# Two-head score pairs in two row halves, and decay rows read back from DRAM, in a two-layer hybrid backbone

## The chip, the cores and the metric

The kernel runs on one core of a Trainium2 chip. The metric is the device time of one execution in microseconds (us). The engines are TensorE (PE, with its weight loads PEld), VectorE (DVE), ScalarE (ACT), GpSimd (POOL) and SyncE (SP), which here issues the DMAs. Each works through its own queue in order.

## The reference, cut to what matters

Two layers over 256 latent and 256 context tokens of 1024 channels, batch 1, all float32. Layer 0 is neighbourhood attention (8 heads of 64) beside a state-space scan (16 heads of 64, 2 groups, state 128, both directions, chunks of 128) and a dense feed-forward; layer 1 is sliding-window attention (8 heads, 2 key heads) beside retention, and a mixture of 8 experts. What the change touches:

```python
s_nb  = einsum('bjqhd,brjkhd->bhjqrk', q_r, k_blk) * scale + bias   # layer 0, contraction over d = 64
s_ctx = einsum('bjqhd,bkhd->bhjqk', q_r, k_ctx) * scale
p = softmax(concat([s_nb, s_ctx]))
...
a_cum = cumsum(a.reshape(b, nc, Q, G, hg), axis=2)                  # Q = 128, a = -dt * exp(a_log)
diff  = a_cum[:, :, :, None] - a_cum[:, :, None, :]
decay_mat = exp(where(causal, diff, -inf))
cb     = einsum('bcign,bcjgn->bcijg', Cr, Br)
y_diag = einsum('bcijg,bcijgh,bcjghp->bcighp', cb, decay_mat, xr)   # xr = x * dt
y_off  = einsum('bcign,bcghpn,bcigh->bcighp', Cr, h_prev, exp(a_cum))
...
yz = (y * silu(z)); yz = yz * rsqrt(mean(yz**2) + EPS) * g          # by group
...
s_loc = where(ok, einsum('bnqkgd,bnskd->bkgnqs', qb, k_win) * scale, -inf)   # layer 1, d = 64
s_ctx = einsum('bnqkgd,bskd->bkgnqs', qb, k_ctx) * scale
```

## The kernel before

Activations lie with channels on partitions (1024 channels are 8 tiles of 128) and 512 tokens (256 latent, 256 context) along the free axis. A float32 product is made of three matmuls on rounded parts, hi·hi, hi·lo and lo·hi (`mm3`, L297 to L299); ScalarE writes the high part (`whi`, L269), VectorE the rest (`wlo`, L270), from weight blocks of 512 KB that SP loads (L276). In time order there are layer 0 (to about 500 us), its feed-forward (to 850), layer 1 (to 1130) and the experts (to the end). A scheduler of the tile framework fixes the order of instructions on each engine when the program is built; on the chip each queue then runs in that order.

Neighbourhood attention, `nattn`, is a generator that is advanced between the input projections. For a pair of heads `t` and each head `hh` of it, `scores` (L632 to L636) makes three matmuls with 64 contraction rows, in the upper or lower half of the array by `hh`, into a bank `ax` of 512 columns (two banks `ax` exist). There are two query tiles of 512 keys and, for the context, two of 256 keys. VectorE adds the bias (L651) and takes the maximum, ScalarE does the exponential, PE transposes (L660, L677), and the product with V follows (L686).

The scan's decay: L732 makes the running sums of `a` as rows of tokens, for both directions and twice over (the second copy holds the low parts). In `ssm2` (L856 to L920), for each pair of heads `pr`, direction `d` and head `hh`, a matmul (L879) copies one of these rows to 128 partitions and 512 tokens (four chunks) in a bank `ax`. Three of the four combinations (`ONACT`) then take ScalarE's Relu with a bias (L884, four times 128x128), an exponential (L889), VectorE's product with the masked `cb` (L890), and a scaling of x by dt on GpSimd (`xd`, L895, four times 128x64); the fourth takes VectorE's add-and-minimum (L887) with dt in the bias and x as it is. Eight matmuls per direction (L900) sum into a bank `pt`, L903 adds `yo` by four transposing matmuls, L905 multiplies with `z`, L910 squares on ScalarE and L912 adds the squares on GpSimd. `cb` comes from L863 and L865, L866. Ahead of `ssm2`, `ssm1` does the convolution's tail and the states (L787 to L824) between the projections of z; after and between the pairs, `out_proj` makes 12 matmuls for each 512-wide output and two residual additions on VectorE (L518). `gnorm` (L853, L270) scales z by group.

Sliding-window attention, `swa` (L1108 to L1146), has the same form as `nattn`, with scores L1120 to L1122. Retention (L1224) already sends the matmuls of two heads to the two row halves in turn.

Of the kernel before, what the change touches and what calls it, by code (L numbers as in the profile page):

```python
# [10 lines left out]
F32 = mybir.dt.float32  # L11
# [7 lines left out]
P = 128  # L19
# [148 lines left out]
def tile_backbone(ctx: ExitStack, tc: tile.TileContext, A, out, upto=99, dbg=None):  # L168
# [7 lines left out]
    ONACT = ((0, 0), (0, 1), (1, 1))  # L176
# [12 lines left out]
    ps = [ps_guard.__enter__()]  # L189
    wp_guard = tc.tile_pool(name="wp", bufs=1)  # L190
# [337 lines left out]
    def layer0():  # L528
# [103 lines left out]
        def scores(o, t, rr, q0, k0, k1):  # L632
            q, k = (q0, q0 + P), (k0, k1)
            T.matmul(o, qH(t, *q)[rr], kH(t, *k)[rr], start=True, stop=False)
            T.matmul(o, qH(t, *q)[rr], kL(t, *k)[rr], start=False, stop=False)
            T.matmul(o, qL(t, *q)[rr], kH(t, *k)[rr], start=False, stop=True)  # L636

        def nattn():
            for t in range(4):
                po = bank("po")  # L640
                ptcs = []
                for hh in range(2):
                    h = 2 * t + hh
                    rr = slice(hh * 64, hh * 64 + 64)
                    bias = pool[0].tile([P, 2, 256], F32, tag="nab", name="nab", bufs=2)
                    nc.sync.dma_start(bias, A["nab"][h].rearrange("p (q k) -> p q k", q=2))
                    PT = pts[hh]
                    for qt in range(2):
                        sc = bank("ax")
                        scores(sc, t, rr, 256 + qt * P, 0, 512)  # L650
                        V.tensor_tensor(sc[:, 256:], sc[:, 256:], bias[:, qt, :], op=ALU.add)  # L651
# [9 lines left out]
                        S.copy(PT[:, :, qt * P:(qt + 1) * P], pt.rearrange("p (t k) -> p t k", t=4))  # L661
                    sc = bank("ax")
                    for qt in range(2):
                        scores(sc[:, qt * 256:qt * 256 + 256], t, rr, qt * P, 0, 256)
# [17 lines left out]
                    if hh == 1:  # L682
                        for c0, n, src in ((256, 4, pts), (0, 2, ptcs)):
                            for kt in range(n):
                                for i in range(2):
                                    T.matmul(po[i * 64:i * 64 + 64, c0:c0 + 256],  # L686
                                             vt[:, kt, (2 * t + i) * 64:(2 * t + i) * 64 + 64], src[i][:, kt, :],
                                             start=kt == 0, stop=kt == n - 1)
                    yield
# [36 lines left out]
        lndt, lnda, acj = ln, x, w1  # L726
        V.tensor_copy(acj, psv[:, :, 0:32])
        V.tensor_tensor(lnda, lndt, psv[:, :, 0:32], op=ALU.subtract)
# [5 lines left out]
        acp = pg([P, 2, 512], "acp", F32R)  # L734
        ac2 = acp[:, 0, :]
        S.activation(ac2[0:64], pac[0:64, :], AF.Copy)
        split(acp[64:128, 1, :], ac2[64:128], pac[64:128, :])
        idr = c1.tile([P, 64], F32R, name="idr")
        for i in range(2):
            V.tensor_copy(idr[64 * i:64 * i + 64], ident[64 * i:64 * i + 64, 64 * i:64 * i + 64])  # L740
# [115 lines left out]
        def ssm2():  # L856
            cbf = pg([P, 4, 2, P], "cbf")
            cbb = pg([P, 4, 2, P], "cbb")
            for g in range(2):
# [5 lines left out]
                V.tensor_tensor(cbf[:, :, g, :], ptv, C("tle")[:, None, :].to_broadcast([P, 4, P]), op=ALU.mult)  # L865
# [1115 lines left out]
```

## Time and profile before

| | us |
|---|---|
| median of 3 runs (lowest, highest) | 2092.88 (2088.6, 2093.2) |
| the profiled execution, its own time | 2092.78 |
| its span | 2091.0 |
| PE busy | 1999.0 (96%) |
| VectorE busy | 1200.4 (57%) |
| ScalarE busy | 833.3 (40%) |
| GpSimd busy | 109.9 (5%) |

The span is the part of an execution that the trace covers; 1.8 us lie around it. Engine times are shares of the span; PE's matmuls overlap one another, so the distance of two starts, not the duration of one, is what a matmul takes from the next. Layer 0's scan lies between about 232 and 409 us, layer 1's windowed attention between 889 and 990.

### The profile page before, as it was taken

How to read it: one execution, taken by the hardware profiler on the slowest of the kernel's cores; microseconds unless marked ns; L12 is line 12 of the kernel's file. 1: busy time of each engine (PE TensorE's matmuls, PEld its weight loads, DVE VectorE, ACT ScalarE, POOL GpSimd, SP SyncE). 2: the span in 40 equal slices, each digit the busy share in tenths (PEclk: the TensorE clock that was granted, in tenths of full speed). 3: DMA queues.
4: the chain of work that ended last, by engine and by line, in shares of the span. 5: the costliest groups of instructions: out<-in, count | busy, mean ns of one | idle time of the engine just before them, and what ended most of it. 6: DMA issues, size and time to landing. Idle time of an engine off the chain costs nothing. (4 is left out here: it accounts for less than half of the span.)

```text
span 2091.0 us, 26240 instructions
## 1 busy us (share of the span) xinstructions
PE 1999.0 (96%) x10002; PEld 1375.9 (66%) x10002; DVE 1200.4 (57%) x1842; ACT 833.3 (40%) x1261; POOL 109.9 (5%) x148
## 2 busy tenths in 40 slices
PE   7999999889999999999999999998999999899997
PEld 4776756688777878888888888855353544444453
DVE  5366557777566664765477888853253343333443
ACT  4346525643222223544356776733132222222221
POOL 0000015600000000100101000000000000000000
PEclk9999999999999999999999999999999999999998
DMA  8423432025444673322253999996999999899994
GB/s 323 149 91 97 150 121 95 27 65 161 142 150 151 211 237 127 125 61 81 82 230 134 332 364 329 319 375 246 419 368 420 392 419 397 350 398 405 396 382 171
DMA packets 89443, 496.22 MB, mean 237 GB/s; under 512 B 10080, under 2 KB 10848, under 8 KB 46048
## 3 DMA queue, kind: packets, MB, share of 16 engines
q1 hardware_dynamic: 89312, 494.49, 63.7%
q8 instruction: 81, 1.33, 0.3%
q14 instruction: 50, 0.41, 0.1%
HBM read 493.40 MB, written 1.05 MB: 236 GB/s over the span
## 5 line engine op out<-in xcount | busy, mean ns | idle before, releaser
L270 DVE TENSOR_TENSOR w<-w 128x2048 fp32r<-128x2048 f32 (+1 forms) x144 | 289.1, 2022 | 78.3 <-ACT w L269 65.8
L269 ACT ACTIVATE whi<-raw 128x1024 fp32r<-128x1024 f32 x151 | 160.0, 1060 | 406.0 <-PE bk_mm L298 264.8
L269 ACT ACTIVATE w<-w 128x2048 fp32r<-128x2048 f32 (+1 forms) x144 | 241.3, 1699 | 71.2 <-DVE w L270 23.1
L270 DVE TENSOR_TENSOR wlo<-raw,whi 128x1024 fp32r<-128x1024 f32 x151 | 186.1, 1233 | 141.5 <-ACT whi L269 139.1
L297 PE MATMUL bk_mm<-fH,whi 128*128 128x512 f32 (+1 forms) x360 | 139.9, 390 | 2.0 <-DVE xT L518 1.2
L299 PE MATMUL bk_mm<-fH,wlo 128*128 128x512 f32 (+1 forms) x360 | 138.9, 387 | 2.1 <-DVE wlo L270 2.1
L1551 PE MATMUL bk_pt<-w,xf 128*64 128x512 f32 x560 | 138.8, 600 | 1.1 <-ACT g L1704 0.6
L297 PE MATMUL bk_mm<-hH,whi 128*128 128x512 f32 (+1 forms) x384 | 137.4, 361 | 2.3 <-ACT hH L269 2.3
L298 PE MATMUL bk_mm<-fL,whi 128*128 128x512 f32 (+1 forms) x360 | 139.2, 388 | 0.0
L298 PE MATMUL bk_mm<-hL,whi 128*128 128x512 f32 (+1 forms) x384 | 136.2, 356 | 0.0
L299 PE MATMUL bk_mm<-hH,wlo 128*128 128x512 f32 (+1 forms) x384 | 135.5, 354 | 0.0
L1763 PE MATMUL bk_mm<-w,gf 128*64 128x512 f32 x560 | 132.5, 598 | 2.2 <-DMA w<-in_m 1.9
L1551 PE MATMUL bk_ax<-w,xf 128*64 128x512 f32 x560 | 132.7, 596 | 0.1
L1704 ACT COPY g<-bk_ax 64x512 f32<-64x512 f32 x42 | 24.5, 582 | 259.5 <-PE bk_ax L1551 259.3
L456 POOL TENSOR_TENSOR rstd<-rstd,mhalf 128x2 f32<-128x2 f32 (+2 forms) x11 | 10.3, 938 | 1493.3 <-DVE rstd L455 1474.2
L1551 PEld LDWEIGHTS bk_ax<-w,xf 128*64 128x64 f32 x560 | 39.2, 137 | 74.7 <-issue 69.7
L1705 DVE TENSOR_TENSOR g<-g,bk_ax 64x512 f32<-64x512 f32 x42 | 28.4, 675 | 101.3 <-ACT g L1704 101.3
L297 PEld LDWEIGHTS bk_mm<-hH,whi 128*128 128x128 f32 x384 | 71.7, 188 | 21.8 <-issue 5.4
L1763 PEld LDWEIGHTS bk_mm<-w,gf 128*64 128x64 f32 x560 | 38.1, 136 | 71.3 <-issue 68.4
L1551 PEld LDWEIGHTS bk_pt<-w,xf 128*64 128x64 f32 x560 | 38.7, 136 | 69.2 <-issue 63.4
L297 PEld LDWEIGHTS bk_mm<-fH,whi 128*128 128x128 f32 x360 | 68.1, 190 | 22.6 <-issue 3.6
L298 PEld LDWEIGHTS bk_mm<-hL,whi 128*128 128x128 f32 x384 | 72.2, 188 | 13.2 <-issue 3.4
(568 smaller groups left out, 4364.3 us busy)
## 6 DMA issues: line engine op xcount, KB each, us to landing
w<-in_m SPq DMA_DIRECT2D x334, 1024.0 KB, 9.5
raw<-in_f SPq DMA_DIRECT2D x66, 512.0 KB, 3.7
araw<-in_adc SPq DMA_DIRECT2D x56, 512.0 KB, 4.0
araw<-in_ada SPq DMA_DIRECT2D x32, 512.0 KB, 7.0
raw<-in_evx SPq DMA_DIRECT2D x29, 512.0 KB, 3.7
raw<-in_odx SPq DMA_DIRECT2D x22, 512.0 KB, 3.6
raw<-in_evo SPq DMA_DIRECT2D x12, 512.0 KB, 3.7
xT<-in_xt SPq DMA_DIRECT2D x4, 1024.0 KB, 5.5
```

Source lines behind the costliest of these rows:

```text
L269: a = S.activation(hi, src, AF.Copy)
L270: v = V.tensor_tensor(lo, src, hi.bitcast(F32), op=ALU.subtract)
L297: T.matmul(o, wh, xh, start=first, stop=False)
L298: T.matmul(o, wh, xl, start=False, stop=False)
L299: T.matmul(o, wl, xh, start=False, stop=last)
L456: G.tensor_tensor(r, r, mhalf[:, :n], op=ALU.pow)
L1551: T.matmul(o[c:c + 64], sl(b[0]), wh, start=k < 2, stop=k >= K - 2, tile_position=(0, c))
L1704: S.copy(g[0:64], hb[b][0][64:128])
L1705: V.tensor_tensor(g[0:64], g[0:64], hb[b][0][0:64], op=ALU.add)
L1763: T.matmul(accs[0][half][64 * q2:64 * q2 + 64], gT[0][0][:, f, :], wh[:, hs], start=first and q == 0, stop=last and q == 1, tile_position= ...
```

## The change

- `scores` takes two banks at once and issues each of its three matmuls for the two heads of a pair, one in the upper, one in the lower row half; `nattn` takes both heads of a query tile, then both heads of the context, and yields three times per pair of heads instead of twice. `swa` is changed in the same way.
- The running sums are made once (half of L732's matmuls go), copied to SBUF by ScalarE, and written to DRAM (`acd`, 64 x 512). In `ssm2` one DMA per pair of heads and direction reads two of these rows back to all 128 partitions (128 x 1024, 512 KB), 16 in all, into one of five buffers E. The 32 matmuls L879 go.
- One minimum on VectorE (128x1024) for two heads takes the place of Relu and add-and-minimum; the exponential is one ScalarE instruction per head and chunk (128x128, 128 in all) with a bias that holds ln dt, so x is used unscaled and GpSimd's 96 scalings go.
- The mask product is 128x1024 for two heads, 16 instead of 32; `cbf` and `cbb` change their layout to fit.
- The sums of squares are added on VectorE (six) and not on GpSimd (five).

```diff
-        def scores(o, t, rr, q0, k0, k1):
+        def scores(os, t, q0, k0, k1):
             q, k = (q0, q0 + P), (k0, k1)
-            T.matmul(o, qH(t, *q)[rr], kH(t, *k)[rr], start=True, stop=False)
-            T.matmul(o, qH(t, *q)[rr], kL(t, *k)[rr], start=False, stop=False)
-            T.matmul(o, qL(t, *q)[rr], kH(t, *k)[rr], start=False, stop=True)
+            for i, (a, b) in enumerate(((qH, kH), (qH, kL), (qL, kH))):
+                for hh, o in enumerate(os):
+                    rr = slice(hh * 64, hh * 64 + 64)
+                    T.matmul(o, a(t, *q)[rr], b(t, *k)[rr], start=i == 0, stop=i == 2)
...
-        for i in range(4):
+        for i in range(2):
             for c in range(4):
                 T.matmul(pac[32 * i:32 * i + 32, c * P:(c + 1) * P], av[:, c, :], C("tge" if i % 2 else "tle"),
                          start=True, stop=True, tile_position=(0, 32 * i))
...
+        acs = pg([P, 2, 512], "acs")[0:64, 0]
+        S.activation(acs, pac[0:64, :], AF.Copy)
+        acd = dr.tile([64, 512], F32, name="acd")
+        nc.sync.dma_start(acd, acs)
...
+            def bcast(n):
+                if n < 16:
+                    sel = n % 2 * 48 + n // 2 * 2
+                    nc.sync.dma_start(Eb[n % 5].rearrange("p a b c -> p (a b c)"),
+                                      acd[sel:sel + 2].rearrange("a b -> (a b)").partition_broadcast(P))
+
+            def clamp(n):
+                o = n % 2 * 16 + n // 2 * 2
+                e = Eb[n % 5].rearrange("p a b c -> p (a b) c")
+                V.tensor_tensor(e, e, acj[:, o:o + 2, :].rearrange("p a b -> p (a b)")[
+                    :, :, None].to_broadcast([P, 8, P]), op=ALU.min)
+
+            for n in range(3):
+                bcast(n)
+            clamp(0)
             for pr in range(8):
...
+                    bcast(2 * pr + d + 3)
+                    if 2 * pr + d + 1 < 16:
+                        clamp(2 * pr + d + 1)
                     for hh in range(2):
                         o = d * 16 + 2 * pr + hh
-                        sel = 32 * d + o
-                        pt = bank("ax")
-                        T.matmul(pt, idr[:, sel:sel + 1].to_broadcast([P, P]), ac2, start=True, stop=True)
                         E = E2[:, hh]
-                        onact = (d, hh) in ONACT
                         for c in range(4):
-                            if onact:
-                                S.activation(E[:, c, :], pt[:, c * P:(c + 1) * P], AF.Relu, scale=-1.0,
-                                             bias=acj[:, c, o:o + 1])
...
-                        S.activation(E, E, AF.Exp, scale=-1.0 if onact else 1.0)
-                        V.tensor_tensor(E, E, (cbb if d else cbf)[:, :, g, :], op=ALU.mult)
...
-                                G.tensor_scalar(xd[:, c, :], xh[c], dt[:, c, o:o + 1], None, op0=ALU.mult)
...
+                            S.activation(E[:, c, :], E[:, c, :], AF.Exp, bias=lnda[:, c, o:o + 1])
+                    V.tensor_tensor(E2.rearrange("p a b c -> p a (b c)"), E2.rearrange("p a b c -> p a (b c)"),
+                                    (cbb if d else cbf)[:, g].rearrange("p b c -> p (b c)")[:, None, :].to_broadcast(
+                                        [P, 2, 512]), op=ALU.mult)
...
-                    G.tensor_tensor(psq[0], psq[0], sq, op=ALU.add)
+                    V.tensor_tensor(psq[0], psq[0], sq, op=ALU.add)
```

Built, the program stands in the following order at three places. Names are tiles: `bk_` a PSUM bank, `hH`, `hL` the layer's normalised input, `nH`, `nL` attention's output, `cbf`, `cbb` the masked products, `Pm` the squares. On PE, at the first scores of `nattn`, between projections, before:

```order
L313 MATMUL bk_ada<-araw,scc 32x512 x2
L634 MATMUL bk_ax<-kH,qH 128x512
L635 MATMUL bk_ax<-kL,qH 128x512
L636 MATMUL bk_ax<-kH,qL 128x512
L634 MATMUL bk_ax<-kH,qH 128x512
L635 MATMUL bk_ax<-kL,qH 128x512
L636 MATMUL bk_ax<-kH,qL 128x512
L297 MATMUL bk_mm<-hH,whi 128x512
```

and now:

```order
L313 MATMUL bk_ada<-araw,scc 32x512 x2
L637 MATMUL bk_ax<-kH,qH 128x512 x2
L637 MATMUL bk_ax<-kL,qH 128x512 x2
L637 MATMUL bk_ax<-kH,qL 128x512 x2
L297 MATMUL bk_mm<-hH,whi 128x512
```

The two of each x2 now belong to the two heads and two banks. Over the program, of the 48 score matmuls with 512 columns in `nattn` 24 stand so beside their partner (12 pairs), of the 48 with 256 columns 34 (17 pairs), and of the 48 of `swa` 40 (20 pairs); the rest stand one head after the other. On PE around `cb` (L863, now L860), where `ssm2` begins, before:

```order
L799 MATMUL bk_ax<-wx,Btok 128x512
L313 MATMUL bk_ada<-araw,scc 32x512
L812 MATMUL bk_ax<-H,CT 128x512 x2
L863 MATMUL bk_ax<-CT,BT 128x128 x4
L313 MATMUL bk_ada<-araw,scc 32x512 x3
L298 MATMUL bk_mm<-nL,whi 128x512
L299 MATMUL bk_mm<-nH,wlo 128x512
L863 MATMUL bk_ax<-CT,BT 128x128 x4
```

and now:

```order
L298 MATMUL bk_mm<-hL,whi 128x512
L299 MATMUL bk_mm<-hH,wlo 128x512
L325 MATMUL bk_ada<-ca,adas 128x128 x4
L860 MATMUL bk_ax<-CT,BT 128x128 x4
L313 MATMUL bk_ada<-araw,scc 32x512 x4
L860 MATMUL bk_ax<-CT,BT 128x128 x4
L297 MATMUL bk_mm<-nH,whi 128x512
```

Before, 46 matmuls of `out_proj` stand ahead of `cb`, among the scan's; now none does, and the scan's states stand among the projections of z (`hH`, `hL`) instead. Ahead of the last L903 (now L904) 132 stood, and 108 stand now. On VectorE in `ssm2`, from the first multiplication with z that follows a masked product, before:

```order
L905 TENSOR_TENSOR z<-z,bk_pt 128x512
L890 TENSOR_TENSOR E<-E,cbf 128x512
L890 TENSOR_TENSOR E<-E,cbb 128x512
L518 SCALAR_TENSOR_TENSOR xT<-bk_mm,mod,xT 128x256 x2
L270 TENSOR_TENSOR wlo<-raw,whi 128x1024
L890 TENSOR_TENSOR E<-E,cbb 128x512
L887 TENSOR_SCALAR E<-bk_ax,dtp 128x128
```

and now:

```order
L906 TENSOR_TENSOR z<-z,bk_pt 128x512
L895 TENSOR_TENSOR E<-E,cbb 128x1024
L876 TENSOR_TENSOR E<-E,dtp 128x1024 x2
L906 TENSOR_TENSOR z<-z,bk_pt 128x512
L895 TENSOR_TENSOR E<-E,cbf 128x1024
L913 TENSOR_TENSOR Pm<-Pm 128x512
```

Minimums (L876) and mask products (L895) now alternate at 128x1024, the minimums up to five buffers ahead, and the additions of squares (L913) stand between them. Four residual additions (L518) stand ahead of the first minimum; they need the first 24 matmuls of `out_proj`. On SP the 16 broadcasts stand in one queue with the loads of the modulation weights (`araw`) of the same stage; the last five loads of out_proj's weights stand behind the last broadcast.

## Rows read from the trace of the kernel before

**Rows 1.** Busy time of each engine by stage (from:to in us, its length, then for PE, PEld, DVE, ACT and POOL the busy time with the number of instructions, PE's granted clock, DMA share, GB/s): attention of layer 0, the scan, `ssm2`, windowed attention of layer 1, the experts.

```profile
115.00:232.00 117.00, 116.47 (x604) 78.93 (x603) 79.64 (x152) 72.50 (x135) 0.00 (x0) 1.00 0.30 98
232.00:336.00 104.00, 102.32 (x433) 65.71 (x432) 64.30 (x102) 28.83 (x52) 15.96 (x20) 1.00 0.40 133
336.00:408.00 72.00, 64.91 (x456) 46.17 (x455) 57.47 (x107) 54.02 (x143) 56.07 (x86) 0.98 0.13 41
...
889.00:990.00 101.00, 100.47 (x703) 85.80 (x702) 64.40 (x155) 46.20 (x102) 6.04 (x5) 1.00 0.23 69
...
1130.00:2091.00 961.00, 908.92 (x4115) 529.57 (x4113) 478.71 (x516) 361.43 (x396) 0.76 (x1) 0.97 0.91 357
```

**Rows 2.** The timeline of PE at the first scores of layer 0 (start, duration, engine, line, operation, tiles, shapes).

```profile
124.66 0.40 PE L297 MATMUL bk_mm<-hH,whi 128*128 128x512 f32 x1
124.89 0.39 PE L298 MATMUL bk_mm<-hL,whi 128*128 128x512 f32 x1
...
126.42 0.50 PE L634 MATMUL bk_ax<-kH,qH 64*128 64x512 f32 x1
126.76 0.39 PE L635 MATMUL bk_ax<-kL,qH 64*128 64x512 f32 x1
126.99 0.39 PE L636 MATMUL bk_ax<-kH,qL 64*128 64x512 f32 x1
```

**Rows 3.** Groups of PE instructions by line and shape in layer 0's attention (count, then busy time, mean ns of one, idle time before them).

```profile
L634 PE MATMUL bk_ax<-kH,qH 64*128 64x512 f32 x16 | 7.7, 484 | 0.0
...
L732 PE MATMUL bk_ax<-ct,dtp 128*32 128x128 f32 x32 | 2.5, 276 | 0.0
```

**Rows 4.** The timeline of PE in layer 1's retention, where scores of two heads are sent to the two row halves; eight instructions are merged to a row.

```profile
999.57 1.70 PE L1224 MATMUL bk_pt<-rq,rk 64*128 64x256 f32 x8 [1.71 <-DVE ktok L1196]
...
1005.83 1.14 PE L1224 MATMUL bk_pt<-rq,rk 64*128 64x256 f32 x8
```

**Rows 5.** Groups of instructions by line and shape between 336 and 408 us (count, busy time, mean ns of one, idle time of the engine just before them and what ended it).

```profile
L895 POOL TENSOR_SCALAR xd<-xtok,dtp 128x64 f32<-128x64 f32 x80 | 48.9, 635 | 8.0 <-PE bk_pt L900 8.0
L884 ACT ACTIVATE E<-bk_ax,dtp 128x128 f32<-128x128 f32 x96 | 28.3, 382 | 10.3 <-PE bk_ax L879 10.1
...
L889 ACT ACTIVATE E<-E 128x512 f32<-128x512 f32 x32 | 19.9, 643 | 1.3 <-DVE E L887 0.9
...
L890 DVE TENSOR_TENSOR E<-E,cbb 128x512 f32<-128x512 f32 x16 | 13.7, 868 | 3.7 <-ACT E L889 3.7
L879 PE MATMUL bk_ax<-acp,idr 128*128 128x512 f32 x32 | 13.4, 453 | 1.2 <-ACT E L884 1.2
L887 DVE TENSOR_SCALAR E<-bk_ax,dtp 128x128 f32<-128x128 f32 x32 | 11.3, 401 | 1.5 <-PE bk_ax L879 1.4
L890 DVE TENSOR_TENSOR E<-E,cbf 128x512 f32<-128x512 f32 x16 | 11.0, 689 | 1.5 <-ACT E L889 1.5
...
L518 DVE SCALAR_TENSOR_TENSOR xT<-bk_mm,mod,xT 128x256 f32<-128x256 f32 x16 | 7.1, 475 | 3.0 <-PE bk_mm L299 3.0
...
L905 DVE TENSOR_TENSOR z<-z,bk_pt 128x512 f32<-128x512 f32 x7 | 4.8, 684 | 3.1 <-PE bk_pt L903 3.1
```

**Rows 6.** Two ends of `ssm2`: from PE's timeline the first matmuls for `cb`, and from the view of line 905 its eight multiplications with z (shortest, median, longest in ns, then the start of the first and of the last).

```profile
331.17 1.16 PE L863 MATMUL bk_ax<-CT,BT 128*128 128x128 f32 x8
...
L905 DVE TENSOR_TENSOR z<-z,bk_pt x8: 673/686/689, 347.6 to 408.7; 128x512 f32<-128x512 f32 x8
```

**Rows 7.** The timeline of VectorE in `ssm2`, where operations follow one another without a wait.

```profile
340.97 0.69 DVE L890 TENSOR_TENSOR E<-E,cbb 128x512 f32<-128x512 f32 x1 [0.18 <-ACT E L889]
341.58 0.68 DVE L890 TENSOR_TENSOR E<-E,cbf 128x512 f32<-128x512 f32 x1
...
343.05 1.22 DVE L270 TENSOR_TENSOR wlo<-raw,whi 128x1024 fp32r<-128x1024 f32 x1
344.18 0.69 DVE L890 TENSOR_TENSOR E<-E,cbb 128x512 f32<-128x512 f32 x1
```

**Rows 8.** The timelines of VectorE and of GpSimd near the end of `ssm2`.

```profile
393.71 2.18 DVE L890 TENSOR_TENSOR E<-E,cbb 128x512 f32<-128x512 f32 x1
...
385.74 8.36 POOL L895 TENSOR_SCALAR xd<-xtok,dtp 128x64 f32<-128x64 f32 x12
394.07 1.28 POOL L912 TENSOR_TENSOR Pm<-Pm 128x512 f32<-128x512 f32 x1
```

**Rows 9.** The timeline of PE after its wait for the last sums of squares of the first group (the time in brackets is the wait), and the granted clock of the 2 us in which it goes on.

```profile
401.91 0.38 PE L840 MATMUL bk_po<-ca,Pm 128*128 128x1 f32 x2 [1.30 <-POOL Pm L912]
...
402.67 0.63 PE L299 MATMUL bk_mm<-yH,wlo 128*128 128x512 f32 x1
403.10 0.63 PE L297 MATMUL bk_mm<-yH,whi 128*128 128x512 f32 x1
...
402.00:404.00 2.00, 2.00 (x7) 1.61 (x8) 1.54 (x2) 0.00 (x0) 0.00 (x0) 0.55 0.05 10
```

**Rows 10.** DMA issues of the whole run (count, KB each, median us from issue to landing), and one row of SP's waits between 240 and 420 us (total, times, longest).

```profile
raw<-in_evx SPq DMA_DIRECT2D x29, 512.0 KB, 3.7
araw<-in_ada SPq DMA_DIRECT2D x32, 512.0 KB, 7.0
row<-in_row SPq DMA_DIRECT2D x1, 36.0 KB, 5.5
...
SPq L416 <- PE bk_ada L313: 6.6, 1, 6.6
```

More of the change, by code (lines that the diff above doesn't have):

```diff
@@ L641, in nattn @@
                 ptcs = []
+                bias = [pool[0].tile([P, 2, 256], F32, tag="nab", name="nab", bufs=2) for _ in range(2)]
                 for hh in range(2):
[L643 to L651, printed above, removed]
+                    nc.sync.dma_start(bias[hh], A["nab"][2 * t + hh].rearrange("p (q k) -> p q k", q=2))
+                for qt in range(2):
+                    scs = [bank("ax") for _ in range(2)]
+                    scores(scs, t, 256 + qt * P, 0, 512)
+                    for hh, sc in enumerate(scs):
+                        V.tensor_tensor(sc[:, 256:], sc[:, 256:], bias[hh][:, qt, :], op=ALU.add)
                         sm = sm_([4], "sm")
@@ L660, in nattn @@
                             T.transpose(pt[:, kt * P:(kt + 1) * P], Pm[:, kt * P:(kt + 1) * P], ident)
[L661 to L664, printed above, removed]
+                        S.copy(pts[hh][:, :, qt * P:(qt + 1) * P], pt.rearrange("p (t k) -> p t k", t=4))
+                    yield
+                scs = [bank("ax") for _ in range(2)]
+                for qt in range(2):
+                    scores([sc[:, qt * 256:qt * 256 + 256] for sc in scs], t, qt * P, 0, 256)
+                for sc in scs:
                     sm = sm_([3, 2], "smc")
@@ L681, in nattn @@
                     ptcs.append(PTc)
[L682 to L689, printed above, removed]
+                for c0, n, src in ((256, 4, pts), (0, 2, ptcs)):
+                    for kt in range(n):
+                        for i in range(2):
+                            T.matmul(po[i * 64:i * 64 + 64, c0:c0 + 256],
+                                     vt[:, kt, (2 * t + i) * 64:(2 * t + i) * 64 + 64], src[i][:, kt, :],
+                                     start=kt == 0, stop=kt == n - 1)
+                yield
                 split(nH(t), nL(t), po)
@@ L725, in layer0 @@
         S.activation(ln, rc, AF.Ln)
-        lndt, lnda, acj = ln, x, w1
-        V.tensor_copy(acj, psv[:, :, 0:32])
-        V.tensor_tensor(lnda, lndt, psv[:, :, 0:32], op=ALU.subtract)
+        lnda, acj = x, w1.rearrange("p a b -> p (a b)").rearrange("p (o c) -> p o c", c=4)
+        V.tensor_copy(acj.rearrange("p o c -> p c o"), psv[:, :, 0:32])
+        V.tensor_tensor(lnda, ln, psv[:, :, 0:32], op=ALU.subtract)
         pac = bank("ax")
-        for i in range(4):
+        for i in range(2):
             for c in range(4):
@@ L856, in ssm2 @@
         def ssm2():
-            cbf = pg([P, 4, 2, P], "cbf")
-            cbb = pg([P, 4, 2, P], "cbb")
+            cbf = pg([P, 2, 4, P], "cbf")
+            cbb = pg([P, 2, 4, P], "cbb")
             for g in range(2):
```

54 lines of the change are left out of this document (18 added, 36 removed).

## The prediction

> **What bounds the kernel now.** I read the stages first [rows 1]. PE is busy 116.5 of 117 us in layer 0's attention and 100.5 of 101 in layer 1's: there the issue of matmuls is the time, VectorE has a third of its time free, and a matmul that goes is time that goes. In `ssm2` (336 to 408) it is otherwise: PE has 7.1 of 72 us idle, and GpSimd is the engine that never rests once it has begun. The groups show why [rows 5]: 80 scalings of x at 0.635 us, and twelve of them, one pair of heads, take 8.36 us [rows 8]. The eight multiplications with z come from 347.6 to 408.7 [rows 6], 8.73 us apart, which is that pace. In the experts DMA has a share of 0.91; nothing there is edited, and their loads start as buffers come free behind layer 1, so I let that stage shift as a block. Clock and profile agree well enough to sum on one execution: 2092.78 us, 2091.0 of span and 1.8 around it, 0.1 below the median.
>
> **Scores of layer 0.** Two matmuls of 512 columns start 0.23 us apart with 128 rows, and also with 64 rows of one head [rows 2]. So half the array gives nothing back today. What two heads in two halves give is seen in retention alone: eight instructions take 1.70 us at the stage's first scores, which followed a wait, and 1.14 further on, where nothing was waited for [rows 4]. Each product there is two instructions on float32, ours is one on rounded parts, so it is the nearest row and not the thing itself. If a pair costs one matmul, the order (12 pairs of 512 columns, 17 of 256) saves 12 × 0.23 + 17 × 0.115 (half of 0.23) = 4.8 us. Entering 64-row tiles costs 0.34 instead of 0.23 [rows 2]; the order has 24 runs of scores where it had 25, so nothing that counts changes there. The other end is zero. The pair also takes both banks `ax` at once: the following scores wait for VectorE and ScalarE to empty both. PE finds projections to do meanwhile, as it does now.
>
> The Trainium skill, "TensorEngine Tiling (Array Packing)", section "PSUM Bottleneck", says that tiling speeds up TensorE but not the emptying of PSUM, which may become the limit. By that rule none of the score term would come; rows 1 speak against it for layer 0, with VectorE at 79.6 and ScalarE at 72.5 of 117 us. That is rival B below.
>
> **Scores of layer 1.** 20 pairs × 0.23 = 4.6 us, less one more run of scores with its 0.11: 4.5. PE fills that stage [rows 1], so it comes off the end. Bounds again zero and 4.5.
>
> **Decay rows, PE's part.** The 32 copies L879 go: 13.4 us busy with waits [rows 5], 32 × 0.23 = 7.4 us of issue. Half of L732 goes: 2.5 / 2 = 1.2 us [rows 3].
>
> **Decay rows, the other engines.** ScalarE: now 28.3 + 19.9 = 48.2 us for E [rows 5]; then 128 × 0.295 (28.3 / 96) = 37.8. GpSimd: its 48.9 us go altogether. VectorE: now 13.7 + 11.0 + 11.3 = 36.0; then 32 operations of 128x1024. Such a one takes 1.22 us, but the next starts 1.13 after it, and 0.61 after one of 512 columns [rows 7]. The whole of VectorE's queue in the new `ssm2`, at these paces: 16 minimums and 16 masks 32 × 1.13 = 36.2; 8 products with z, 6 additions of squares and 8 operations of `gnorm`, 22 × 0.61 = 13.4; four `wlo` 4.5; 16 residual additions × 0.475 = 7.6 [rows 5]; small ones 2. Sum 63.7 us, some 8.0 per pair. ScalarE with 37.8 and eight squares has room, PE too (108 matmuls of out_proj, 25 us, and about 25 of the scan). **So VectorE is late next**, and the stage runs nearly as long as it did under GpSimd. What it gains is the start.
>
> **Where the stage starts.** `cb` came at 331.2 [rows 6]. Ahead of it go 46 matmuls of out_proj (46 × 0.23 = 10.6), 4.8 of scores and 1.2 of L732: 314.6. Then `cb` itself 2 us (eight instructions 1.16, twice) and the 24 matmuls for which four residual additions at the head of VectorE's queue wait, 5.5: 322.1. The scan lies closer to the z projections now; its VectorE chain may hold PE up. Bounds zero and 7 us; VectorE had 64.3 of 104 us [rows 1], which leaves room, so I take 2: 324.1.
>
> **Where it ends.** To the 63.7 come VectorE's waits: today 3.7 + 1.5 + 1.5 + 3.0 + 3.1 = 12.8 [rows 5], under a stage bound elsewhere; an engine that is the bound waits less. Bounds zero and 12.8, taken 6.4. Last product with z: 324.1 + 63.7 + 6.4 = 394.2, and its end was 409.4 (408.7 + 0.7). The 24 matmuls that now stand behind it (132 less 108) are 5.5 us more after it. Layer 0 gains 15.2 - 5.5 = **9.7 us**.
>
> As a second reading, PE alone: 4.8 + 1.2 + 7.4 = 13.4 us of issue go from layer 0, and if PE's stalls stay, that is the gain. VectorE's sum is the later one, so I take it.
>
> **Squares on VectorE.** Six additions are in the sum. GpSimd's addition did harm where it ran: the mask product at 393.71 took 2.18 us beside the one at 394.07 [rows 8], 0.69 otherwise; the other product, 0.868 against 0.689 in the mean [rows 5], has such cases in it, 16 × 0.18 = 2.9 us. Beside the scalings it ran at 0.68 to 0.69 [rows 7]. My sum has the undisturbed pace already. The Trainium skill, "GPSIMD Engine Reference", section "Key points", says that GpSimd shares its SBUF interfaces with VectorE and contends with operations that have two SBUF inputs. By it all 32 products would have been slowed by the scalings and get faster now; rows 7 disagree for scalings and rows 8 agree for additions, so nothing more than the 2.9 is to be had.
>
> **DMA.** Each broadcast is 512 KB. Loads of that size land in 3.7 to 7.0 us, and the one load that reads one row for all partitions, 36 KB, in 5.5 [rows 10]. A buffer's round is eight matmuls (1), landing, a minimum (1.2), eight exponentials (2.4), a mask product (1.2): 5.8 us and the landing, for five steps of (63.7 + 6.4) / 16 = 4.4 us. The landing is hidden up to 22 - 5.8 = 16 us. On SP's queue a broadcast can stand behind a load that waits for PE, 6.6 us at the worst [rows 10]: 13.6, still hidden. I take zero.
>
> **Sum.** 2092.8 - 4.5 - 9.7 = 2078.6.
>
> **The rivals.**
> B, the pairs give nothing (rounded matmuls of two halves don't overlap, or both banks empty too late). For it: no such pair is in the trace. Against it: rows 4. Price: 4.8 + 4.5, 2088.
> C, slower: the ring of E is bound by the broadcasts. All 128 partitions read the same 4 KB, which no row of that size shows. From a landing of 16 us on, each us adds 0.2 to a step. To eat the 14.2 and lose 0.3% besides takes 20.5 us, 1.3 a step, so a landing of 22.5, three times the longest row: about 2100.
> D, PE stays the bound: VectorE waits less, PE's stalls shrink. At PE's 13.4 it is 2074.9; with its 7.1 idle us of `ssm2` gone too, 2068.
> E, VectorE waits as much as now and the scan holds up by 7 us: layer 0 loses 6.4 + 5 of its 9.7, so 2090.
> A smaller one goes into the bounds: after 1.30 us of idle PE, two matmuls started 0.43 apart instead of 0.23, at a granted clock of 0.55 in these 2 us, nearly all of them at the lower of its two levels, 1.2 and 2.4 GHz [rows 9]. PE will have more gaps in the new `ssm2`; eight matmuls so are 1.6 us.
>
> **How the numbers follow.** The forecast with its own bounds (waits zero to 12.8, 2074 to 2086) has 0.52, D 0.18 (2066 to 2074), B 0.12, E 0.08, C 0.10. A measurement here tells about 0.3%, 6.3 us, from no change: faster means below 2086.5. Faster 0.70, same 0.20 (B, E), slower 0.10 (C). The range from 2067 to 2091 leaves out C and a little of D.
>
> **What would show it.** Row-half scores right: pairs of L637 start together, 0.23 to the next pair, and attention of layer 1 is shorter by some 4.5 us; wrong: partners 0.23 apart. Stage right: first `cb` near 315, VectorE busy nine tenths up to a last product with z near 394, few waits of L876 on a DMA; GpSimd empty. Wrong: L876 waits for broadcasts (C), or PE is full and VectorE waits for it (D), or `cb` later than 322 (E). The sum fails too if a minimum with a repeated operand is slower than 1.22 us: 0.3 more each is 5 us.

## The result

| | us |
|---|---|
| before, median of 4 runs (lowest, highest) | 2093.04 (2088.6, 2094.52) |
| changed, median of 4 runs (lowest, highest) | 2075.03 (2072.48, 2076.72) |
| ratio, 95% interval | 0.9909 [0.9895, 0.9924] |
| forecast | 2078.6 (2067 to 2091) |
| profiled execution of the changed kernel; its span | 2076.72; 2075.0 |

The change makes the kernel 18.0 us faster by the medians, 16.1 by the two profiled executions; 14.2 were forecast. The engines, from the profile page of the changed kernel (busy us, share of the span, instructions):

```profile
PE 1981.0 (95%) x9954; PEld 1365.9 (66%) x9954; DVE 1201.5 (58%) x1812; ACT 835.2 (40%) x1266; POOL 47.8 (2%) x47
```

GpSimd lost the 62 us of its scalings and additions, PE 18. The stages of layer 0, at the times of [rows 1] and with its columns:

```profile
232.00:336.00 104.00, 100.56 (x466) 64.67 (x468) 70.43 (x110) 42.22 (x96) 9.90 (x4) 0.97 0.43 152
336.00:408.00 72.00, 63.03 (x453) 47.49 (x454) 61.48 (x85) 42.71 (x115) 2.93 (x2) 0.93 0.42 141
```

The last stage of the scan now begins inside the first window and VectorE has 61.5 of 72 us in the second. Its two ends, in the views of [rows 6] (the lines have moved):

```profile
L860 PE MATMUL bk_ax<-CT,BT x16: 275/275/377, 309.7 to 312.6; 128*128 128x128 f32 x16
```

```profile
L906 DVE TENSOR_TENSOR z<-z,bk_pt x8: 677/688/689, 336.0 to 389.7; 128x512 f32<-128x512 f32 x8
```

`cb` comes 21.5 us earlier (309.7 for 331.2) and the last product with z 19.0 (389.7 for 408.7). By the starts of the first matmuls of each stage, the feed-forward begins 13.3 us earlier (439.7 for 453.0), the windowed attention too (875.6 for 889.0), retention 16.9 (982.7 for 999.6), and the end comes 16.0 earlier. So layer 0 brought 13.3 of the 16.0 us, and layer 1 2.7.

The paired scores, from PE's timeline at the place of [rows 2]; two matmuls are merged to a row:

```profile
126.10 0.50 PE L637 MATMUL bk_ax<-kH,qH 64*128 64x512 f32 x2
126.44 0.40 PE L637 MATMUL bk_ax<-kL,qH 64*128 64x512 f32 x2
126.67 0.39 PE L637 MATMUL bk_ax<-kH,qL 64*128 64x512 f32 x2
126.99 0.50 PE L297 MATMUL bk_mm<-hH,whi 128*128 128x512 f32 x1
```

The second row of two matmuls starts 0.34 us after the first and the third 0.23 after the second, exactly as single ones did in [rows 2]. From start to start, all scores of layer 0 took 21.65 us before and 16.71 now, those of layer 1 13.13 and 8.67: 4.9 and 4.5 us, where 4.8 and 4.5 were worked out.

VectorE's groups between 320.5 and 390.4 us (columns as in [rows 5]):

```profile
L876 DVE TENSOR_TENSOR E<-E,dtp 128x1024 f32<-128x1024 f32 x16 | 19.4, 1216 | 0.4 <-DMA E<-acd 0.4
L895 DVE TENSOR_TENSOR E<-E,cbf 128x1024 f32<-128x1024 f32 x8 | 9.7, 1216 | 0.0
...
L518 DVE SCALAR_TENSOR_TENSOR xT<-bk_mm,mod,xT 128x256 f32<-128x256 f32 x15 | 6.6, 475 | 4.2 <-PE bk_mm L299 4.2
L906 DVE TENSOR_TENSOR z<-z,bk_pt 128x512 f32<-128x512 f32 x8 | 5.5, 687 | 5.7 <-PE bk_pt L904 5.7
```

The minimum and the mask product take 1.216 us each, as was taken from [rows 7]; only 0.4 us of waiting is put down to a broadcast. From the page and from the view of the line that issues them, the broadcasts (count, KB, median us to landing; then shortest, median, longest):

```profile
E<-acd SPq DMA_DIRECT2D x16, 512.0 KB, 4.2
```

```profile
DMA to landing us min/median/max: 3.3/4.2/10.5
```

PE and VectorE in stretches of 10 us of that stage (columns as in [rows 1]):

```profile
320.00:330.00 10.00, 7.30 (x37) 5.86 (x38) 9.24 (x11) 9.45 (x27) 0.00 (x0) 0.91 0.82 326
330.00:340.00 10.00, 10.00 (x83) 6.61 (x80) 7.01 (x9) 6.52 (x21) 0.00 (x0) 0.74 0.60 180
...
370.00:380.00 10.00, 3.04 (x21) 2.03 (x20) 9.75 (x13) 6.86 (x19) 0.00 (x0) 0.63 0.00 1
380.00:390.00 10.00, 9.57 (x78) 7.75 (x78) 9.09 (x11) 4.32 (x14) 0.00 (x0) 0.86 0.24 64
```

Between 370 and 380 VectorE is full and PE busy for 3.0 of 10 us: VectorE has taken GpSimd's place. PE's granted clock falls to its lower level, 1.2 of 2.4 GHz, for 6.8 us from 328.3, near the end of a wait of 2.7 us for the first mask product, and for 10.2 us from 372.7.

### The profile page after: what moved, and what is told of

It reads as the page before. It is cut to its first block, busy times and chain, and to the rows that moved or that the text cites. A ratio compares the mean times of both kernels' runs of the same rounds, so it can differ in the third digit from the quotient of the medians.

```text
span 2075.0 us, 26034 instructions
## 1 busy us (share of the span) xinstructions
PE 1981.0 (95%) x9954; PEld 1365.9 (66%) x9954; DVE 1201.5 (58%) x1812; ACT 835.2 (40%) x1266; POOL 47.8 (2%) x47
## 5 line engine op out<-in xcount | busy, mean ns | idle before, releaser
L298 PEld LDWEIGHTS bk_mm<-hL,whi 128*128 128x128 f32 x384 | 73.4, 191 | 14.2 <-issue 4.9
L299 PEld LDWEIGHTS bk_mm<-hH,wlo 128*128 128x128 f32 x384 | 73.4, 191 | 12.2 <-issue 3.1
```

The source lines that it names most:

```text
L298: T.matmul(o, wh, xl, start=False, stop=False)
L299: T.matmul(o, wl, xh, start=False, stop=last)
```

## The experiments

The main theory is the forecast's: pairs save PE's issue in both layers, the decay part lets the last stage of the scan start earlier, and VectorE then sets its pace. The first rival is PE: its 13.4 us of issue gone from layer 0 agree with the 13.3 that layer 0 gained, better than the forecast's 9.7 do. The second is that an engine other than these two, or the clock, sets the pace.

**Each part alone.** First the kernel before with the scores of the changed one (both `scores`/`nattn` and `swa`), then the changed kernel with the scores of before.

```diff
-                        sc = bank("ax")
-                        scores(sc, t, rr, 256 + qt * P, 0, 512)
+                    scs = [bank("ax") for _ in range(2)]
+                    scores(scs, t, 256 + qt * P, 0, 512)
```

This is the first, against the kernel before; the second is the same turned round, against the changed kernel.

> The kernel before with the paired scores of both layers and nothing else of the change. Its order on PE outside the scores is that of before. If a pair in two row halves costs one matmul and PE's issue is the time in both stages, 4.9 + 4.5 us come off the end: 2093.0 - 9.4 = 2083.6. If the two banks taken at once or the emptying of PSUM eats it, 2090 or more. If VectorE or the clock gives part of it back in the stages behind, between the two.

> The changed kernel with the scores of before, so the decay part alone. If the two parts add, 18.0 - 9.4 = 8.6 us are left: 2084.4. If the decay part made more (its earlier start of the stage, 21.5 us in the trace) and the scores less than they save in issue, 2080 or less; if it lives from the scores' time, 2090.

Measured: scores alone 0.9964 [0.9953, 0.9974] (2084.7 for 2094.9 in the same series), the decay part alone 0.9928 [0.9905, 0.9952] (2077.4). By its ratio the first is 7.5 us (0.0036 of 2093), between its cases; by the two medians it would be 10.2, its first case. Its trace has 7.3 up to retention's first scores (992.2 for 999.6). The second is 15 us by its ratio where 8.6 were expected if the parts add; its case of 2080 or less holds. The first `cb` and the products with z, of the scores alone:

```profile
L863 PE MATMUL bk_ax<-CT,BT x16: 270/275/377, 327.8 to 331.2; 128*128 128x128 f32 x16
```

```profile
L905 DVE TENSOR_TENSOR z<-z,bk_pt x8: 673/687/690, 344.2 to 404.8; 128x512 f32<-128x512 f32 x8
```

and of the decay part alone:

```profile
L860 PE MATMUL bk_ax<-CT,BT x16: 275/275/377, 311.8 to 314.6; 128*128 128x128 f32 x16
```

```profile
L906 DVE TENSOR_TENSOR z<-z,bk_pt x8: 676/686/687, 335.4 to 389.3; 128x512 f32<-128x512 f32 x8
```

Alone, the pairs of layer 0 bring `cb` 3.4 us forward and the feed-forward 3.8 (449.2), of 4.9 us of issue. With the decay part in, they bring `cb` 2.1 us forward (309.7 for 311.8), but the last product with z comes at 389.7 with them and at 389.3 without: layer 0 ends at 439.7 and 439.3. In these two executions the lead is gone at the end of layer 0; where it goes is told below. In layer 1 the pairs bring the same either way: from the first score to retention's first it takes 107.0 us with pairs in the scores alone, 107.1 in the changed kernel, and 110.5 without in both kernels.

**Pairs with the heads one after the other.** Both banks are still taken at once.

```diff
-            for i, (a, b) in enumerate(((qH, kH), (qH, kL), (qL, kH))):
-                for hh, o in enumerate(os):
+            for hh, o in enumerate(os):
+                for i, (a, b) in enumerate(((qH, kH), (qH, kL), (qL, kH))):
```

> The changed kernel, still with both banks taken at once, but the three matmuls of one head ahead of the three of the other, so no two neighbours lie in different halves (but one in the middle of each six). If the overlap of neighbours is what gives, nearly all of the 9.4 us are lost, less one neighbouring pair in each set: between 2080 and 2084. If the new order of the softmax around them gives it, 2075.

Measured: 0.9908 [0.9890, 0.9926], 2073.7 us. It isn't the test that it was made for: the scheduler put most partners side by side again (20 pairs of 29 in layer 0, 18 of 20 in layer 1), as PE's timeline of this kernel has it:

```profile
125.50 0.51 PE L637 MATMUL bk_ax<-kH,qH 64*128 64x512 f32 x2
125.84 0.41 PE L637 MATMUL bk_ax<-kL,qH 64*128 64x512 f32 x2
```

All scores of layer 0 took 17.94 us in it, those of layer 1 9.20, so 1.23 and 0.53 more than in the changed kernel. The pairs that were parted, two of 512 and seven of 256 columns in layer 0 and two of 512 in layer 1, make 1.27 and 0.46 at 0.23 and 0.115 us each. So where partners were parted, with both banks still taken at once, the time came back. That the overlap is what saves rests on these distances in the timelines; the median, no longer than the changed kernel's, doesn't tell 1.8 us.

**More work for VectorE, more for PE.** The minimum made twice; and a float32 matmul more in each step.

```diff
                 V.tensor_tensor(e, e, acj[:, o:o + 2, :].rearrange("p a b -> p (a b)")[
                     :, :, None].to_broadcast([P, 8, P]), op=ALU.min)
+                V.tensor_tensor(e, e, acj[:, o:o + 2, :].rearrange("p a b -> p (a b)")[
+                    :, :, None].to_broadcast([P, 8, P]), op=ALU.min)
```

```diff
                     bcast(2 * pr + d + 3)
+                    T.matmul(bank("ax"), BT[:, g, 0:P], CT[:, g, :], start=True, stop=True)
```

> The changed kernel with every minimum made twice (the second changes nothing): 16 more operations of 1.13 us on VectorE, 18.1 us, and nothing more on PE. If VectorE sets the pace of the scan's last stage, 12 to 18 us longer: 2087 to 2093. If PE does, with or without its low clock, 2080 or less.

> The changed kernel with one matmul more for each of the 16 steps of the scan's last stage: float32, 128x512, into a bank that nobody reads, two instructions of 0.43 us as in the state products of the same trace, 13.8 us on PE in all. If VectorE sets the pace, 0 to 4 us longer (2075 to 2079), or shorter where the filled gaps keep the clock up. If PE with its low clock does, 10 us or more: 2085.

Measured: the doubled minimum takes 2096.4 us (1.0015 [1.0003, 1.0027]), 21 more than the changed kernel and more than the 12 to 18 expected; the added matmuls 2074.8 (0.9915 [0.9898, 0.9933]), nothing more. The products with z of the two:

```profile
L908 DVE TENSOR_TENSOR z<-z,bk_pt x8: 677/687/689, 336.4 to 406.4; 128x512 f32<-128x512 f32 x8
```

```profile
L907 DVE TENSOR_TENSOR z<-z,bk_pt x8: 681/686/687, 334.0 to 389.7; 128x512 f32<-128x512 f32 x8
```

Of 18.1 us added to VectorE's queue 16.7 arrive at the last product and 16.6 at the feed-forward (456.3 for 439.7); what the time has beyond that came behind layer 0, where nothing was edited. Of 13.8 added to PE none arrive in the sum. Two stretches of the second kernel:

```profile
330.00:340.00 10.00, 10.00 (x101) 6.66 (x98) 8.84 (x11) 9.76 (x32) 0.00 (x0) 1.00 0.79 268
...
370.00:380.00 10.00, 9.64 (x58) 5.98 (x52) 9.67 (x15) 6.53 (x16) 0.00 (x0) 1.00 0.02 7
```

With the gaps filled, PE's clock stays at its upper level through the stage, and the last product comes at 389.7 all the same. Taken apart, this execution is 2.0 us ahead at the fourth mask product (334.7 for 336.6), where the changed kernel had the low clock, and takes 2.0 longer from there (55.1 for 53.1 to the last product). So some 2 of the 13.8 us arrive at most, which refutes the first rival: VectorE was the time. That the low clock of the later part cost next to nothing is seen elsewhere. From the fourth mask product to the last product with z it is 53.1 us in the changed kernel, with 10.2 us of low clock, and 53.2, 52.9 and 52.7 in the decay part alone, the kernel with layer 1 unpaired and the one with the heads one after the other, which have the same order on VectorE there and 6.8 us of it.

**Less work for VectorE, more for ScalarE.** Six of the 16 minimums by Relu on ScalarE; and the same with the unpaired scores in layer 0.

```diff
+            RL = (5, 7, 9, 11, 13, 15)
             def clamp(n):
                 o = n % 2 * 16 + n // 2 * 2
+                if n in RL:
+                    for hh in range(2):
+                        for c in range(4):
+                            S.activation(Eb[n % 5][:, hh, c, :], Eb[n % 5][:, hh, c, :], AF.Relu, scale=-1.0,
+                                         bias=acj[:, o + hh, c:c + 1])
+                    return
```

> The changed kernel with 6 of the 16 minimums (steps 5, 7, 9, 11, 13, 15) made by ScalarE as eight Relu each, as the kernel before had it: VectorE 6 x 1.13 = 6.8 us less, ScalarE 48 x 0.29 = 13.9 us more. If VectorE sets the pace, 4 to 7 us shorter: 2068 to 2071. If PE does, 2075. If ScalarE comes last then, longer than 2075.

> As the kernel with 6 Relu steps, but with the scores of layer 0 of before; layer 1's stay paired. With VectorE as the limit, the 4.9 us of PE issue that pairs save in layer 0 were of no use, since the scan's last stage ended at the same time with and without them. If that is the reason, they come to light with VectorE relieved: 2 to 5 us longer than the kernel with pairs. If the pairs lose their time in the attention itself, 1 us or less.

Measured: 2083.4 us (0.9947 [0.9928, 0.9966]) and 2086.4 (0.9967 [0.9958, 0.9977]). The third of the three expected cases holds for the first: ScalarE comes last. A stretch of it, and its products with z, then those of the second kernel:

```profile
360.00:370.00 10.00, 5.83 (x63) 4.21 (x64) 8.94 (x12) 9.90 (x32) 1.90 (x1) 0.90 0.35 115
```

```profile
L916 DVE TENSOR_TENSOR z<-z,bk_pt x8: 687/688/690, 332.9 to 394.7; 128x512 f32<-128x512 f32 x8
```

```profile
L916 DVE TENSOR_TENSOR z<-z,bk_pt x8: 686/689/689, 337.3 to 399.5; 128x512 f32<-128x512 f32 x8
```

A step with Relu costs ScalarE 8 × 0.29 more, 2.3 us on top of its 2.3, against 4.4 us between steps. The whole stretch from 350 to 390, with Relu and then in the changed kernel:

```profile
350.00:390.00 40.00, 26.39 (x210) 20.87 (x209) 28.22 (x37) 36.46 (x114) 1.93 (x1) 0.77 0.23 74
```

```profile
350.00:390.00 40.00, 32.38 (x262) 24.81 (x260) 37.78 (x49) 26.62 (x75) 1.92 (x1) 0.87 0.34 113
```

With Relu ScalarE is busy 36.5 of 40 us and VectorE 28.2; in the changed kernel ScalarE has a third of its time free. So ScalarE becomes the limit under this load, which doesn't make it the next limit of the changed kernel.

Without pairs, the feed-forward begins 4.6 us later (454.0 for 449.4); by the times, 3.0 us apart with overlapping intervals, the two kernels aren't told apart. Of the 4.6 us 3.2 stand at `cb` (312.4 for 309.2), and 1.3 come between the first and the fourth mask product, where the clock is low for 3.4 us in this execution and not in the other. So it isn't the attention that loses the pairs' lead. VectorE's relief, for which the run was meant, isn't shown as the reason, since another engine was the bound in it and the clocks differ.

**Where the pairs' lead goes.** The timelines answer it. The first mask product starts at 327.6 in the changed kernel and 329.7 in the decay part alone, the full 2.1 us; the fourth at 336.6 and 336.0, and from there both take 53 us to the last product. Between them VectorE waits for the first product with z in the changed kernel and not in the decay part alone:

```profile
336.01 0.69 DVE L906 TENSOR_TENSOR z<-z,bk_pt 128x512 f32<-128x512 f32 x1 [2.59 <-PE bk_pt L904]
```

```profile
335.44 0.69 DVE L906 TENSOR_TENSOR z<-z,bk_pt 128x512 f32<-128x512 f32 x1
```

The 8 us ahead of these products, in the same two kernels (columns as in [rows 1], the clock third from the end):

```profile
328.00:336.00 8.00, 7.11 (x50) 4.67 (x52) 5.42 (x7) 5.24 (x18) 0.00 (x0) 0.57 0.27 77
```

```profile
330.00:338.00 8.00, 6.87 (x71) 4.92 (x71) 8.00 (x10) 7.14 (x25) 0.00 (x0) 1.00 0.53 158
```

PE waits 2.7 us for the first mask product in both. From the first to the fourth mask product it then takes 9.0 us where the clock is low for 6.8 us (the changed kernel), 7.7 to 7.8 in three executions where it is low for 3.4 us (the heads one after the other, Relu without pairs, and layer 1 unpaired, which is the next experiment), and 6.4 in four where it doesn't fall (the decay part alone, Relu, and the two other kernels of the next experiment). So the stretch is worth 2.6 us, and the pairs' 2.1 us went into it. (The doubled minimum and the added matmul change the work there.) The kernel with layer 1 unpaired has the same order in layer 0 as the changed one: its last product comes at 387.2, 2.0 us ahead of the decay part alone, and its feed-forward at 437.3 (439.3). `cb` itself comes at 308.7 to 311.2 in seven executions with the same order up to it, so a difference of 2 us between two executions is near that spread. Why the clock falls in one execution and not in another stays open.

**Layer 1 unpaired, the squares elsewhere.** The scores of `swa` of before; the additions back on GpSimd; the squares summed on PE block by block. In the last, and in the last kernel of the next experiment, the sums of squares of a group come out other than the reference's, and with them the scale of z; for the time alone they are used here.

```diff
-                    for i, (a, b) in enumerate(((qH, kH), (qH, kL), (qL, kH))):
...
+                        T.matmul(sc, qH[rr, t, q], kH[rr], start=True, stop=False)
```

```diff
-                    V.tensor_tensor(psq[0], psq[0], sq, op=ALU.add)
+                    G.tensor_tensor(psq[0], psq[0], sq, op=ALU.add)
```

```diff
-                    V.tensor_tensor(psq[0], psq[0], sq, op=ALU.add)
...
+                T.matmul(bks[pr // 4][:, t:t + 1], sq[:, t * P:(t + 1) * P], ones[:, 0:1],
+                         start=pr % 4 == 0, stop=pr % 4 == 3, skip_group_check=True)
```

> The changed kernel with the scores of layer 1 of before. By the forecast's term 4.5 us longer, 2079.5; by the traces so far, in which the pairs shorten the stage by 3.5 us and retention behind it now and then loses 3.1 to a low clock, 0 to 3.5 us longer: 2075 to 2078.5.

> The changed kernel with the additions of squares back on GpSimd: 6 x 0.61 = 3.7 us less on VectorE, and five additions of 1.27 us beside which operations of VectorE were stretched by 0.5 to 1.5 us before. If the contention is worth the move, 2075 to 2079; if not, 2071 to 2074.

> The changed kernel without the additions of squares: each squared block goes at once into PE's sums over channels (64 instructions of one column in all instead of the 16 for two added blocks and their rest), so VectorE has 6 x 0.61 = 3.7 us less. If VectorE sets the pace, 2 to 4 us shorter: 2071 to 2073. If another limit is near, 2075.

Measured: 2080.4 us (0.9941 [0.9922, 0.9959]), 2078.5 (0.9930 [0.9911, 0.9948]) and 2076.6 (0.9927 [0.9906, 0.9948]). All three intervals overlap that of the changed kernel, so no more than a direction is told by the times; the first is nearest to the case with the forecast's 4.5. In the traces, layer 1's stage is 110.6 us without pairs, 3.5 more. GpSimd's additions stretch VectorE again: in that kernel, VectorE and GpSimd,

```profile
352.47 1.96 DVE L895 TENSOR_TENSOR E<-E,cbb 128x1024 f32<-128x1024 f32 x1
```

```profile
352.05 1.30 POOL L913 TENSOR_TENSOR Pm<-Pm 128x512 f32<-128x512 f32 x1 [8.82 <-ACT Pm L911]
```

a mask product of 1.96 us beside the addition; another takes 2.31 beside the addition at 386.62, the others 1.22. The last product with z comes at 392.3, 2.6 us later, of which 1.5 was there at `cb` (311.2, by execution), though the clock doesn't fall at the stage's start: from the fourth mask product on it takes 56.8 us for 53.1. With the additions on neither, 3.7 us less for VectorE, it comes at 388.7, 1.0 earlier, of which 0.9 was there at `cb` (308.8): nothing gained, and the expectation was wrong. From the first mask product to the end of the last product with z VectorE is busy 52.9 us and idle 9.8 in it; in the kernel with layer 1 unpaired, where `cb` comes at 308.7, 55.4 and 5.9. What it doesn't add it waits: 1.5 us more for the modulation's product on PE, 1.2 for the scale of the first group, the rest in small amounts, none of it put down to ScalarE. Adding to VectorE costs nearly all, taking from it here gives nothing. What is left to try is the start.

**The start of the stage.** In the changed kernel SP's queue has, ahead of the first broadcasts:

```profile
303.38 8.53 SPq L276 DMA_DIRECT2D raw<-in_evo  x2
312.00 0.86 SPq L383 DMA_DIRECT2D araw<-in_ad  x2
312.90 2.39 SPq L870 DMA_DIRECT2D E<-acd  x5
```

two weight loads that wait for a buffer until VectorE has made a `wlo`, from 310.3 to 311.6. The rows have been in DRAM since 122.6 (written at 120.3, landed 2.3 later). The first broadcast lands at 319.0. VectorE doesn't wait for it, since its first minimum stands behind the residual additions:

```profile
320.76 0.88 DVE L518 SCALAR_TENSOR_TENSOR xT<-bk_mm,mod,xT 128x256 f32<-128x256 f32 x2 [4.23 <-PE bk_mm L299]
321.55 1.22 DVE L876 TENSOR_TENSOR E<-E,dtp 128x1024 f32<-128x1024 f32 x1
```

So both had to move: the first three broadcasts and the first minimum were written ahead of `cb`; then the same with the squares on PE.

```diff
         def ssm2():
+            Eb = [pg([P, 2, 4, P], "E") for _ in range(5)]
+            def bcast(n):
...
+            for n in range(3):
+                bcast(n)
+            clamp(0)
             cbf = pg([P, 2, 4, P], "cbf")
...
             yield
-            Eb = [pg([P, 2, 4, P], "E") for _ in range(5)]
...
-            for n in range(3):
-                bcast(n)
-            clamp(0)
             for pr in range(8):
```

> The changed kernel with the first three broadcasts and the first minimum written ahead of cb instead of behind it. In the order the first broadcasts then stand ahead of two loads of weights, on which SP's queue waits 8.5 us, and the first masks stand right behind cb, ahead of all but none of the residual additions for which VectorE waits 5.7 us. If the start of the stage is what it waits for, 6 to 10 us shorter: 2065 to 2069. If VectorE's sum or the ring of buffers sets the end whatever the start, 2075.

> Both of the last two edits together, the early start and the squares summed on PE. If they add, 8 to 14 us shorter than the changed kernel: 2061 to 2067. If either takes the other's place, as the early start alone.

Measured: the early start 2067.5 us (0.9880 [0.9862, 0.9898]), the fastest of all, 7.5 under the changed kernel by the medians and 6.1 by the ratios, whose intervals touch; its slowest run (2068.8) is 3.7 faster than the fastest of the changed kernel (2072.5). Both together take 2078.4 (0.9933 [0.9913, 0.9953]), which fits neither of its cases. The mask products and the products with z of the early start:

```profile
L896 DVE TENSOR_TENSOR E<-E,cbf x8: 1215/1218/1219, 311.7 to 374.8; 128x1024 f32<-128x1024 f32 x8
```

```profile
L907 DVE TENSOR_TENSOR z<-z,bk_pt x8: 679/686/689, 320.9 to 382.1; 128x512 f32<-128x512 f32 x8
```

The first mask product comes at 311.7 and not 327.6, the last product with z at 382.1, and the feed-forward begins at 432.1 (439.7), with `cb` only 0.9 earlier (308.8). Of 15.9 us of earlier start 7.6 are left at the end; VectorE's sum has to be worked off all the same. Part of the 7.6 is the low clock at the start of the changed kernel's stage, which this execution hasn't: against the kernel with layer 1 unpaired, with `cb` at 308.7 as here, the feed-forward begins 5.1 us earlier (437.3). The run moves the broadcasts and the minimum together and doesn't tell one from the other. With the squares on PE as well, the feed-forward begins at 439.7 again. VectorE is idle 19.2 us instead of 8.8 between the first mask product and the last product with z, most of it in waits for the residual additions, which the scheduler placed otherwise; of both together, then of the early start alone:

```profile
DVE xT L518 <- PE bk_mm L299: 9.1, 4, 4.1
```

```profile
DVE xT L518 <- PE bk_mm L299: 2.2, 3, 1.0
```

## Why the prediction was right

**Pairs.** Right as to issue, 4.9 and 4.5 us for 4.8 and 4.5 (12 × 0.23 + 17 × 0.115 is 4.7, not 4.8); rival B falls by the timeline. In layer 1 the stage gave 3.5 of the 4.5 us. The sum took layer 0's 4.8 whole off the start of the stage and so off the end: alone they gave 3.4 at `cb` and 3.8 at the feed-forward, and beside the decay part 2.1 at `cb`, which the low clock then took in the profiled execution. About a fifth of the issue saved is lost in either layer when nothing else is changed. The Trainium skill's rule that tiling speeds up TensorE but not the emptying of PSUM ("TensorEngine Tiling (Array Packing)", section "PSUM Bottleneck") is no account of it in layer 0: between 100 us and `cb` PE is idle 1.6 us with the pairs alone and 2.2 before. What is lost there lies in the distance of neighbours: 80 matmuls of the modulation (L313) take 15.8 us from start to start with pairs and 13.8 without. In layer 1 PE idles 0.6 us more with pairs, which may be emptying; no run separates it.

**The start.** `cb` was put at 314.6 and came at 309.7. The term that was too small is what moves behind `cb`: the 46 matmuls of out_proj were counted, the modulation's (L313) weren't. Between 232 us and `cb`, in the kernel before,

```profile
L313 PE MATMUL bk_ada<-araw,scc 128*32 128x512 f32 x50 | 9.5, 605 | 0.5 <-DMA araw<-in_ad 0.5
```

and in the changed one

```profile
L313 PE MATMUL bk_ada<-araw,scc 128*32 128x512 f32 x24 | 4.2, 605 | 0.0
```

26 fewer, 9.5 - 4.2 = 5.3 us. They stand in the scan's last stage now, where PE's time is nearly free, as the added matmuls showed. The traces of before and of the decay part alone, from start to start, assign the 19.4 us that it brings at `cb`: 11.8 are out_proj (forecast 10.6), 6.2 the modulation, 0.9 the running sums (2.39 before, 1.46 now, 1.2 forecast) and 3.4 the scan's own products (L799 and L812, 20.2 and 16.8), less 2.8 that the products with `hH` and `hL` take more. From `cb` to the second pair of residual additions it took 11.1 us, put at 7.5 and 2 for a hold-up; so VectorE's queue began 3.3 us ahead of the forecast and not 4.9.

**VectorE late next.** Right. Its queue was put from 324.1 to 394.2, 70.1 us; it ran from 320.8, the second pair of residual additions, to 390.4: 69.6. Its waits in it, taken as 6.4 with 12.8 as the bound, were 7.3, of them 5.7 for products with z; the 4.2 at the head of the queue are in the forecast's start. The 13.4 us of PE alone, which agree better with layer 0's 13.3, are a coincidence: 13.8 us more on PE made the kernel no longer.

**The end of layer 0.** From the last product with z to the feed-forward it took 44.3 us before and 50.0 now: 5.7 for the 24 matmuls that stand behind it, 5.5 forecast.

**DMA.** Rival C falls: 4.2 us of landing, 0.4 of waiting. What the forecast didn't see is that the first five, issued within 2 us, take up to 10.5, and that SP's queue holds them until 312.9. In the changed kernel neither cost more than those 0.4 us, as the first minimum stands behind the residual additions; moved up together with it, they were worth 5 to 7.5 us.

**Squares.** Right in direction: GpSimd's additions stretch VectorE's products with two inputs, its scalings hardly did: in the kernel before, 24 mask products beside scalings alone took 0.67 to 0.79 us, five beside nothing 0.68 to 0.69. The rule of the Trainium skill ("GPSIMD Engine Reference", section "Key points") holds for the additions, 1.96 us for 1.22, and not for the scalings.

**What layer 1 gave back.** Retention's scores took 24.0 us from the first to the last before and 27.1 now. There the clock fell at 983.6 for 6.8 us; in the execution with added matmuls, whose layer 1 is the same program, it didn't, and they took 24.0. The changed kernel, then that one:

```profile
984.00:988.00 4.00, 4.00 (x17) 3.35 (x16) 2.30 (x3) 0.45 (x1) 0.00 (x0) 0.50 0.27 69
```

```profile
984.00:988.00 4.00, 4.00 (x33) 3.65 (x31) 3.04 (x4) 2.01 (x3) 0.12 (x1) 1.00 0.25 61
```

17 matmuls instead of 33 in the same 4 us: 3.1 us by one execution's clock, nearly the whole 3.5 of layer 1's pairs. It isn't the pairs' doing: with layer 1 unpaired retention's scores took 27.1 us too, with 6.8 us of low clock. Behind retention 2.3 us came back. There PE, VectorE and ScalarE have the same instructions in the same order in all fourteen kernels traced, and from retention's last score to the end these take 1064.0 to 1067.6 us, so 2.3 is no more than two executions differ by. Layer 1 shows 3.5 - 3.1 + 2.3 = 2.7 us and not 4.5, and two of the three terms belong to the executions and not to the change. The median lies 1.7 us under the profiled execution.

**How near by luck.** The mechanism held in all its parts, but that the sum came within 4 us is luck in part: `cb` 4.9 us earlier than put, 1.6 us more from `cb` to VectorE's queue, and 2.6 and 3.1 us lost to a clock that the forecast had in its bounds alone, with 1.6.

## What to carry to other kernels

When work leaves one stage, read where the scheduler puts everything else, not only the edited lines: of the 19.4 us by which the decay part alone moved the stage's first matmuls, 18.0 came from instructions that merely changed places. Test a limit by loading each engine in turn, since taking away from the bound shows only the waits behind it. Before two savings are said not to add, compare the clock in the same stretch of several executions: here 6.8 us of low clock ate the 2.1 us that pairs had brought. A transfer whose data is ready early is worth issuing ahead of loads that wait for a buffer, if the first operation on it moves up too: here moving three DMAs and a minimum up by some lines brought 5 to 7.5 us.

## What was not expected of the hardware

Two row halves overlap fully for matmuls on rounded parts: six matmuls of 512 columns, three pairs, lie from 126.10 to 126.99, 0.89 us, where six single ones lay from 126.42 to 128.01, 1.59 us, and entering and leaving the mode is in both. What a low clock of PE costs goes by the stretch: where PE fed VectorE at the stage's start 2.6 us for 6.8 us at half the rate (1.3 for 3.4), in retention 3.1 for 6.8, and where VectorE was full no more than 0.4 for 3.4 us more of it. With the same program it came in one execution and not in another.
